# Four buffers for weight halves, gate columns carried in the first z group, v and o groups 512 wide, Q and K normalised together

## The chip, the core and the metric

One Trainium2 chip, one of its cores. The metric is device microseconds of one execution of the whole program: the median of several executions, beside one more execution that is profiled.

## What is computed

One layer of a hybrid decoder over 256 tokens of width 2048, in float32. Four mixers run side by side on slices of one projection, then an output projection, then a SwiGLU block:

```python
def rmsnorm(x, w): return x * rsqrt(mean(x * x, -1) + eps) * w

u = rmsnorm(x, attn_norm) @ w_in          # w_in: 2048 x 6928
u_gdn, u_mlstm, u_rglru, u_rwkv = split(u)
# gated delta net: silu(conv(q, k, v)), l2norm(q), l2norm(k), gates a_raw, b_raw (4 + 4 columns),
#   chunkwise delta rule (a triangular solve per chunk), rmsnorm(o) * silu(z)
# mLSTM: silu(conv(q, k)), v, o, gates i_raw, f_raw (4 + 4 columns), rmsnorm(sigmoid(o) * h)
x = x + concat([y_gdn, y_mlstm, y_rglru, y_rwkv], -1) @ w_out      # 2048 x 2048
n = rmsnorm(x, ffn_norm)
x = x + (silu(n @ ffn_w_gate) * (n @ ffn_w_up)) @ ffn_w_down       # hidden 5632
return rmsnorm(x, final_norm)
```

## The kernel before

**Products in halves.** A float32 operand is split into a high part, rounded to the float32r format, and the rest as a low part. `mm3` (lines 169 to 171) makes one product of three matmuls: high x high, high x low, low x high. Weights come in units of 128 x 1024 float32 (512 KB). One unit goes through three engines: SP's queue loads it into a `raw` buffer (4 of them), ACT copies it to `whi`, DVE subtracts to `wlo` (3 of each), all recorded at line 274 because one helper issues them.

**Groups.** `group` (line 374) makes 256 columns of the input projection from four units: 96 matmuls that move 256 columns each, into one PSUM bank (`big`). The order in the program is: low-rank and R0, K0, V0, R1, K1, V1 of RWKV, four groups of RG-LRU, then of the gated delta net z0, Q0, K0, V0, z1, Q1, K1, V1, then of mLSTM v0, o0, q0, k0, v1, o1, q1, k1. Then come `w_out` and the feed-forward part, whose groups are 512 wide with two banks.

**Mixers.** The mixers are generators (`rwkv_half`, `rglru_half`, `gdn_half`, `mlstm_half`, `joint_solve`). `spawn` registers one, and `tick` lets each live generator take a step, 0.65 steps for each unit of weights. So their small matmuls (L409 products, L413 transposes, through `Lag`, with a lower priority) stand among the 96 matmuls of the groups. The order of each engine is fixed when the program is built: a scheduler with priorities lists it, and on the chip every engine goes through its list in that order and waits where an operand is not there. A buffer of a pool (`slots`: A, B and L of 2 KB a partition, D of 4 KB) that is still in use also makes an instruction wait, or move back in the list.

**The gates.** `gates_mm` makes the 16 gate columns of both mixers in a product of its own: 48 matmuls `mx<-nhi,sA` of 16 output rows and 256 columns.

**The delta rule's end.** `gdn_half` goes, after the triangular solve, through two chunks in turn: products with the state (L409), a subtract (L985), further products, squares for the norm (ACT L990), a power (POOL L993), the product with z's gate (L996) and the new state (L1019); then L413 transposes and a last ACT copy (L1038). mLSTM's half likewise makes K x Q, a product with a decay (L1065), products with V, and ends in POOL L1088 and transposes. `w_out` takes the eight parts in the order rw, rg, gd (`early`), for four column blocks q, and then ml (`late`); `split` (L1178 on ACT, L1179 on DVE) halves each part where it is first needed.

## Time and profile before

| | us |
|---|---|
| median of 3 executions | 1277.48 (1275.78 to 1279.14) |
| the profiled execution | 1275.4 |
| its span, first to last instruction | 1273.4 |
| TensorE (PE) busy in the span | 1241.5 |
| DVE (VectorE) busy | 780.7 |
| ACT (ScalarE) busy | 633.6 |
| POOL (GpSimd) busy | 112.3 |

2.0 us of the profiled execution lie around its span. Busy time of PE counts matmuls that stand in its pipeline, so PE can be busy and still not at its peak. A granted clock (PEclk) of 1.00 is 2.4 GHz; 0.51 is its lower level, 1.2 GHz. Groups of rows from the trace name an operation as out<-in by the names of the program, without numbers of buffers.

### The profile page before, as it was taken

The numbers are of one execution on the slowest core, as the hardware profiler recorded it, in microseconds if no ns is written. First come the engines' busy times: TensorE is split into PE (matmuls) and PEld (weight loads), VectorE is DVE, ScalarE is ACT, GpSimd is POOL, SyncE is SP. The second block draws the span as 40 slices with busy tenths as digits, with TensorE's granted clock in tenths as the row PEclk, the third lists the DMA queues.
The fourth block names the chain that finished last, engine by engine and source line by source line (L and its number), as shares of the span: only waits on it lengthen the run. The fifth ranks groups of instructions, "written<-read, shape, count | busy, mean of one in ns | idle before, by whom it ended". The sixth has DMA issues, their size and how long they took to land.

```text
span 1273.4 us, 18370 instructions
## 1 busy us (share of the span) xinstructions
PE 1241.5 (98%) x7216; PEld 1072.9 (84%) x7216; DVE 780.7 (61%) x1045; ACT 633.6 (50%) x831; POOL 112.3 (9%) x123
## 2 busy tenths in 40 slices
PE   9899999999899999999999999999999999999997
PEld 8788999988899788888888888888888888888885
DVE  7885799665689775744444444454445455557554
ACT  7664684526643454644444344444444444445443
POOL 1520210212401020000000000000000000001000
PEclk9999999999898999999999999999999999999999
DMA  8554436445455356566666666666666666666663
GB/s 320 187 169 133 143 109 191 136 127 160 134 169 156 117 166 191 176 189 188 187 194 189 190 191 206 199 194 191 190 186 197 185 185 194 198 191 190 197 190 125
DMA packets 72198, 226.97 MB, mean 178 GB/s; under 512 B 15752, under 2 KB 16016, under 8 KB 72112
## 3 DMA queue, kind: packets, MB, share of 16 engines
q1 hardware_dynamic: 71504, 224.14, 57.5%
q0 software_dynamic: 464, 1.57, 0.4%
q8 instruction: 56, 0.92, 0.3%
q14 instruction: 30, 0.25, 0.1%
q10 hardware_dynamic: 144, 0.10, 0.0%
HBM read 222.49 MB, written 3.28 MB: 177 GB/s over the span
## 4 chain that ended last, share of the span: by engine, by line
PE 85%; DVE 8%; issue 2%; ACT 2%; DMA 1%; POOL 1%; DVEq 0%; POOLq 0%; SPq 0%; ACTq 0%
PE big L171 13%; PE big L170 13%; PE big L169 13%; PE mx L170 10%; PE mx L171 10%; PE mx L169 10%; PE mx L409 4%; PE mxl L169 3%; PE mxl L171 3%; PE mxl L170 3%; DVE wlo L274 3%; PE big L277 2%; DVE sD L499 1%; DVE sD L500 1%; DVE sA L763 1%
## 5 line engine op out<-in xcount | busy, mean ns | idle before, releaser
L274 DVE TENSOR_TENSOR wlo<-raw,whi 128x1024 fp32r<-128x1024 f32 x396 | 488.4, 1234 | 375.0 <-ACT whi L274 374.0
L274 ACT ACTIVATE whi<-raw 128x1024 fp32r<-128x1024 f32 x396 | 418.7, 1057 | 456.3 <-PE big L171 280.6
L170 PE MATMUL big<-wlo,nhi 128*128 128x512 f32 (+1 forms) x464 | 163.3, 352 | 3.6 <-DVE wlo L274 3.6
L169 PE MATMUL big<-whi,nhi 128*128 128x512 f32 (+1 forms) x464 | 162.1, 349 | 0.7 <-ACT whi L274 0.7
L171 PE MATMUL big<-whi,nlo 128*128 128x512 f32 (+1 forms) x464 | 162.4, 350 | 0.0
L171 PE MATMUL big<-nhi,wlo 128*128 128x256 f32 x544 | 157.8, 290 | 3.6 <-DVE wlo L274 3.6
L170 PE MATMUL big<-nlo,whi 128*128 128x256 f32 x544 | 158.1, 291 | 0.0
L169 PE MATMUL big<-nhi,whi 128*128 128x256 f32 x544 | 157.6, 290 | 0.0
L169 PE MATMUL mx<-whi,nhi 128*128 128x512 f32 x352 | 138.0, 392 | 0.0
L171 PE MATMUL mx<-whi,nlo 128*128 128x512 f32 x352 | 137.0, 389 | 0.0
L170 PE MATMUL mx<-wlo,nhi 128*128 128x512 f32 x352 | 137.0, 389 | 0.0
L171 PEld LDWEIGHTS big<-nhi,wlo 128*128 128x128 f32 x544 | 104.9, 193 | 6.0 <-DVE wlo L274 4.4
L170 PEld LDWEIGHTS big<-nlo,whi 128*128 128x128 f32 x544 | 105.1, 193 | 2.2 <-issue 1.0
L169 PEld LDWEIGHTS big<-nhi,whi 128*128 128x128 f32 x544 | 105.0, 193 | 1.9 <-issue 0.7
L170 PEld LDWEIGHTS big<-wlo,nhi 128*128 128x128 f32 x464 | 89.7, 193 | 15.2 <-DVE wlo L274 4.0
L169 PEld LDWEIGHTS big<-whi,nhi 128*128 128x128 f32 x464 | 89.5, 193 | 11.6 <-ACT whi L274 0.9
L171 PEld LDWEIGHTS big<-whi,nlo 128*128 128x128 f32 x464 | 89.7, 193 | 10.8
L170 PE MATMUL mx<-wlo,sA 128*128 128x512 f32 x216 | 84.3, 390 | 0.1
L169 PE MATMUL mx<-whi,sA 128*128 128x512 f32 x216 | 84.4, 391 | 0.0
L171 PE MATMUL mx<-whi,sA 128*128 128x512 f32 x212 | 82.5, 389 | 0.0
L171 PEld LDWEIGHTS mx<-whi,nlo 128*128 128x128 f32 x352 | 66.1, 188 | 13.8
L170 PEld LDWEIGHTS mx<-wlo,nhi 128*128 128x128 f32 x352 | 66.1, 188 | 13.3
...
## 6 DMA issues: line engine op xcount, KB each, us to landing
...
```

Source lines behind the costliest of these rows:

```text
L169: i = nc.tensor.matmul(out, ahi, bhi, start=start, stop=False, skip_group_check=True)
L170: nc.tensor.matmul(out, ahi, blo, start=False, stop=False, skip_group_check=True)
L171: self.last_mm = nc.tensor.matmul(out, alo, bhi, start=False, stop=stop, skip_group_check=True)
L274: i = fn(*a, **k)
L277: i = fn(*a, **k)
L409: return self.em.nc.tensor.matmul(*a, **k)
L499: nc.vector.tensor_tensor(tv, col, row, op=ALU.mult)
L500: nc.vector.tensor_tensor(inv[:, j + 1 : n, 0:b], inv[:, j + 1 : n, 0:b], tv, op=ALU.add)
L763: nc.vector.scalar_tensor_tensor(o[:, d:T], u[:, 0 : T - d], tap[3 - d], o[:, d:T], op0=ALU.mult, op1=ALU.add)
```

## The change

Five edits. (1) `NHI` goes from 3 to 4: a fourth `whi` and `wlo`, paid with two A and two B slots. (2) The 16 gate columns are appended to the weights of the group z0, which becomes 272 wide, in six units of three or two K tiles (`token_group`, tokens as output rows); `gates_mm` now copies 16 columns out of each of the two banks and transposes them. (3) The mLSTM's v and o are made by two groups 512 wide for both halves, in place of four of 256, and ahead of them stand q0 and k0. (4) In `gdn_half`, Q's and K's normalisation run side by side, so that the two Ln stand together and the two Exp. (5) In `w_out`, a part is split one turn ahead of its use (`ready`), and ml's two parts before the late pass.

```diff
@@ -29,8 +29,8 @@
-SLOTS = dict(A=14, B=13, L=4, D=16)
-NRAW, NHI = 4, 3
+SLOTS = dict(A=12, B=11, L=4, D=16)
+NRAW, NHI = 4, 4
 
 
 RW, RG, GD, ML = OFF_RW, OFF_RG, OFF_GDN, OFF_ML
...
@@ -40,14 +40,20 @@
+ZG = GD + 1536
+ZG_UNITS = ((0, 3), (3, 3), (6, 3), (9, 3), (12, 2), (14, 2))
 
 
 def plan():
 
     units = []
-    cols = [RW + c for c in range(0, 1792, 256)] + [RG + c for c in range(0, 1024, 256)] + [o + c for o in (GD, ML) for c in range(0, 2048, 256)]
+    cols = [RW + c for c in range(0, 1792, 256)] + [RG + c for c in range(0, 1024, 256)] + [GD + c for c in range(0, 2048, 256)] + [ML + c for c in range(0, 1024, 256)]
     for c in cols:
-        units += [("w_in", k, 4, c, 256) for k in range(0, KT, 4)]
+        if c == ZG:
+            units += [("z_gates", k, nk, c, 272) for k, nk in ZG_UNITS]
+        else:
+            units += [("w_in", k, 4, c, 256) for k in range(0, KT, 4)]
+    units += [("w_in", k, 2, ML + c, 512) for c in (1024, 1536) for k in range(0, KT, 2)]
     units += [("w_out", k, 2, c, 512) for c in range(0, D, 512) for k in range(0, KT, 2)]
     for c in range(0, HID, 512):
         units += [(w, k, 2, c, 512) for w in ("ffn_w_gate", "ffn_w_up") for k in range(0, KT, 2)]
...
@@ -370,6 +377,22 @@
+
+    def token_group(self, name, col, n, units, pre=None):
+
+        banks = [self.bank(), self.bank()]
+        for u, (k0, nk) in enumerate(units):
+            w = self.weights(name, k0, nk, col, n)
+            if pre:
+                pre(u)
+            for a in range(2):
+                ts = slice(a * P, a * P + P)
+                for kk in range(nk):
+                    k = k0 + kk
+                    self.mm3(banks[a][:, 0:n], self.nhi[:, k, ts], self.nlo[:, k, ts], w[0][:, kk, :], w[1][:, kk, :], start=k == 0, stop=k == KT - 1)
+            if self.gens:
+                self.tick(TICKS * nk * n / UNIT)
+        return banks
 
     def group(self, name, col, tm=False, acts=None, pre=None):
 
...
@@ -770,37 +793,35 @@
...
-def gates_mm(em):
+def gates_mm(em, zg):
     nc = em.nc
-    gs = em.S()
-    ghi, glo = (gs.bitcast(F32R)[:, i * 256 : i * 256 + 256].rearrange("p (k n) -> p k n", k=KT) for i in range(2))
-    nc.scalar.activation(ghi, em.gw, AF.Copy)
-    nc.vector.tensor_tensor(glo, em.gw, ghi.bitcast(F32), op=ALU.subtract)
+    gt = em.S()
+    with em.tc.high_priority(offset=EPRIO):
+        for a in range(2):
+            nc.vector.tensor_copy(gt[:, a * 16 : a * 16 + 16], zg[a][:, 256:272])
     z = em.mx()
     o = z[0:16, 0:T]
-    for k in range(KT):
-        em.mm3(o, ghi[:, k, :], glo[:, k, :], em.nhi[:, k, :], em.nlo[:, k, :], start=k == 0, stop=k == KT - 1)
-    em.free(gs)
+    for a in range(2):
+        em.pe.transpose(z[0:16, a * P : a * P + P], gt[:, a * 16 : a * 16 + 16], em.ident)
+    em.free(gt)
     g = em.S(2)
     gp = em.gp
     U, V = g[0:16, 0:T], g[0:16, T : 2 * T]
...
@@ -870,15 +890,30 @@
     nc = em.nc
     KQ = em.S(2)
     KQv = KQ.rearrange("p (s n) -> p s n", s=2)
-    for s, X, bias in ((1, Q, em.c_lnq), (0, K, 0.0)):
+    sqs, parts = [], []
+    for X in (Q, K):
         silu2(em, X)
-        sq = em.S()
-        nc.scalar.activation(sq, X, AF.Square)
-        z = yield from sums(em, em.onesr, sq)
-        rsqrt_ln(em, sq, z, em.c_4eps, ebias=bias)
+    for X in (Q, K):
+        sqs.append(em.S())
+        nc.scalar.activation(sqs[-1], X, AF.Square)
+    for sq in sqs:
+        parts.append((em.S(c="B"), em.S(c="B")))
+        nc.scalar.activation(parts[-1][0].bitcast(F32R), sq, AF.Copy)
+        nc.gpsimd.tensor_tensor(parts[-1][1].bitcast(F32R), sq, parts[-1][0], op=ALU.subtract)
+    yield
+    zs = []
+    for p in parts:
+        zs.append(em.mx())
+        for i in range(2):
+            em.pe.matmul(zs[-1], em.onesr, p[i].bitcast(F32R), start=i == 0, stop=i == 1)
+        em.free(*p)
+    for sq, z in zip(sqs, zs):
+        nc.scalar.activation(sq, z, AF.Ln, bias=em.c_4eps)
+    for s, X, sq, bias in ((1, Q, sqs[0], em.c_lnq), (0, K, sqs[1], 0.0)):
+        nc.scalar.activation(sq, sq, AF.Exp, scale=-0.5, bias=bias)
         nc.vector.tensor_tensor(KQv[:, s, :], X, sq, op=ALU.mult)
         em.free(sq, X)
-        yield
+    yield
     silu2(em, V)
     z = em.mx()
     for u in range(4):
...
@@ -1192,14 +1227,19 @@
     row = {"gd": 0, "ml": 4, "rg": 8, "rw": 12}
     sp = {}
 
+    def ready(m, hf):
+        if (m, hf) not in sp:
+            while (m, hf) not in em.mix:
+                em.tick()
+            sp[m, hf] = split(em, em.mix[m, hf])
+            em.free(em.mix[m, hf])
+
     def run(q, parts):
         banks = [em.bank(), em.bank()]
         for i, (m, hf) in enumerate(parts):
-            if (m, hf) not in sp:
-                while (m, hf) not in em.mix:
-                    em.tick()
-                sp[m, hf] = split(em, em.mix[m, hf])
-                em.free(em.mix[m, hf])
+            ready(m, hf)
+            if (m, hf) in early and q == 0 and i + 1 < len(early):
+                ready(*early[i + 1])
             hi, lo = (t.bitcast(F32R) for t in sp[m, hf])
             whi, wlo = em.weights("w_out", row[m] + 2 * hf, 2, q * 512, 512)
             for a in range(2):
...
@@ -1216,6 +1256,9 @@
     late = [("ml", 0), ("ml", 1)]
     for q in range(4):
         run(q, early)
+        if q == 2:
+            ready("ml", 0)
+    ready("ml", 1)
     ss = em.const([P, 2, 4], "ss1")
 
     def norm(q):
...
@@ -1409,31 +1439,41 @@
                 Gt = gelu2(em, grp(RG + 512 + 256 * hf))
                 em.spawn(f"rg{hf}", rglru_half(em, hf, X, Gt, wax))
         if "gd" in parts or "ml" in parts:
-            em.spawn("gates", gates_mm(em))
             em.gnh = em.const([P, 1], "gnh")
             nc.vector.tensor_scalar(em.gnh, em.PT["gdn_norm"], 0.5, None, op0=ALU.mult)
         if "gd" in parts:
             for hf in range(2):
-                z = grp(GD + 1536 + 256 * hf, tm=True)
                 SZ = em.S(c="L")
-                silu2(em, SZ, z)
+                if hf == 0:
+                    zg = em.token_group("z_gates", ZG, 272, ZG_UNITS)
+                    for a in range(2):
+                        silu2(em, SZ[:, a * T : a * T + T], zg[a][:, 0:T])
+                    em.spawn("gates", gates_mm(em, zg))
+                else:
+                    silu2(em, SZ, grp(ZG + 256, tm=True))
                 Q, K, V = (conv(em, grp(GD + 512 * i + 256 * hf), em.PT["gdn_conv"], 12, (4 * i + 2 * hf, 4 * i + 2 * hf + 1)) for i in range(3))
                 em.spawn(f"gd{hf}", gdn_half(em, hf, Q, K, V, SZ))
                 if hf == 0:
                     em.spawn("gds", joint_solve(em, "gd", 64, 32, 8, True))
         if "ml" in parts:
+            qk = [conv(em, grp(ML + 512 * i), em.PT["mlstm_conv"], 8, (4 * i, 4 * i + 1)) for i in range(2)]
+            v1s = [em.S(2) for _ in range(2)]
+            V1 = [t[:, 0:516].rearrange("p (a h n) -> p a h n", a=2, h=2) for t in v1s]
+            b = em.token_group("w_in", ML + 1024, 512, PAIRS)
             for hf in range(2):
-                v1s = em.S(2)
-                V1 = v1s[:, 0:516].rearrange("p (a h n) -> p a h n", a=2, h=2)
-                nc.gpsimd.memset(V1[:, :, :, 128:129], 1.0)
-                b = grp(ML + 1024 + 256 * hf, tm=True)
-                nc.scalar.activation(V1[:, :, :, 0:128], b.rearrange("p (a h n) -> p a h n", a=2, h=2), AF.Copy)
-                b = grp(ML + 1536 + 256 * hf, tm=True)
-                SO = em.S(c="L")
-                nc.scalar.activation(SO, b, AF.Tanh, scale=0.5)
-                nc.vector.tensor_scalar(SO, SO, 0.5, 0.5, op0=ALU.mult, op1=ALU.add)
-                Q, K = (conv(em, grp(ML + 512 * i + 256 * hf), em.PT["mlstm_conv"], 8, (4 * i + 2 * hf, 4 * i + 2 * hf + 1)) for i in range(2))
-                em.spawn(f"ml{hf}", mlstm_half(em, hf, Q, K, V1, SO, v1s))
+                nc.gpsimd.memset(V1[hf][:, :, :, 128:129], 1.0)
+                for a in range(2):
+                    nc.scalar.activation(V1[hf][:, a, :, 0:128], b[a][:, hf * T : hf * T + T].rearrange("p (h n) -> p h n", h=2), AF.Copy)
+            b = em.token_group("w_in", ML + 1536, 512, PAIRS)
+            SO = [em.S(c="L") for _ in range(2)]
+            for hf in range(2):
+                for a in range(2):
+                    nc.scalar.activation(SO[hf][:, a * T : a * T + T], b[a][:, hf * T : hf * T + T], AF.Tanh, scale=0.5)
+                nc.vector.tensor_scalar(SO[hf], SO[hf], 0.5, 0.5, op0=ALU.mult, op1=ALU.add)
+            for hf in range(2):
+                if hf:
+                    qk = [conv(em, grp(ML + 512 * i + 256), em.PT["mlstm_conv"], 8, (4 * i + 2, 4 * i + 3)) for i in range(2)]
+                em.spawn(f"ml{hf}", mlstm_half(em, hf, *qk, V1[hf], SO[hf], v1s[hf]))
```

`token_group` replaces the feed-forward part's own nested `group`, with the same matmuls; `silu2` takes narrower sources. Each unit is loaded with as many columns as it has.

On PE, in the delta net's first z group (nhi, nlo: the halves of the normalised tokens; mx_2045: the gates' bank; sA_275: the gates' weight halves), the order before is:

```order
L169 MATMUL big_1980<-whi_1983,nhi 128x256
L170 MATMUL big_1980<-wlo_1984,nhi 128x256
L171 MATMUL big_1980<-whi_1983,nlo 128x256
L409 MATMUL mx_2021<-sA_243_1799,sD_162_1283 128x256 x2
L409 MATMUL mx_2026<-sA_243_1799,sD_162_1283 128x256
L169 MATMUL mx_2045<-nhi,sA_275_2042 16x256
L170 MATMUL mx_2045<-nlo,sA_275_2042 16x256
L171 MATMUL mx_2045<-nhi,sA_275_2042 16x256
```

and of the change, at the same place:

```order
L176 MATMUL big_1980<-whi_1983,nhi 128x272
L177 MATMUL big_1980<-wlo_1984,nhi 128x272
L178 MATMUL big_1980<-whi_1983,nlo 128x272
L176 MATMUL big_1979<-whi_2007,nhi 128x272
L177 MATMUL big_1979<-wlo_2008,nhi 128x272
L178 MATMUL big_1979<-whi_2007,nlo 128x272
```

The 48 rows of 16x256 are gone, and the 96 of the group are 272 wide.

On ACT, where the RWKV's last norm runs (sB_448, sB_451 before, sB_455, sB_458 after; mx: the sums it takes its roots of; in mLSTM's first group before), the order before is:

```order
L486 ACT_TABLE_LOAD
L486 ACTIVATE sB_448_3516<-mx_3638,cv 128x512
L759 ACTIVATE sA_473_3648<-big_3485,chan 128x256
L487 ACT_TABLE_LOAD
L487 ACTIVATE sB_448_3516<-sB_448_3516 128x512
L486 ACT_TABLE_LOAD
L486 ACTIVATE sB_451_3522<-mx_3643,cv 128x512
L274 ACTIVATE whi_3793<-raw_3791 128x1024
L487 ACT_TABLE_LOAD
L487 ACTIVATE sB_451_3522<-sB_451_3522 128x512
L274 ACTIVATE whi_3825<-raw_3823 128x1024
```

and of the change:

```order
L509 ACT_TABLE_LOAD
L509 ACTIVATE sB_455_3484<-mx_3606,cv 128x512
L509 ACTIVATE sB_458_3490<-mx_3611,cv 128x512
L782 ACTIVATE sA_480_3616<-big_3453,chan 128x256
L510 ACT_TABLE_LOAD
L510 ACTIVATE sB_455_3484<-sB_455_3484 128x512
L510 ACTIVATE sB_458_3490<-sB_458_3490 128x512
L898 ACTIVATE sA_488_3673<-sA_430_3260 128x512
L898 ACTIVATE sA_489_3675<-sA_450_3444 128x512
L901 ACTIVATE sB_490_3677<-sA_488_3673 128x512
L281 ACTIVATE whi_3799<-raw_3797 128x1024
```

Four table loads among the RWKV norm's rows have become two; two more follow for the delta net's half in either kernel.

On PE, where the delta net's chain ends and the output projection begins (big_4901, big_4648: the bank of k1; big_5113, big_4893: the first of w_out; mx: the mixers' banks), before:

```order
L171 MATMUL big_4901<-nhi,wlo_5046 128x256
L409 MATMUL mx_5021<-sA_652_4936,sD_361_2834 128x128 x2
L409 MATMUL mx_5026<-sB_505_3861,sA_575_4427 128x128
L169 MATMUL big_5113<-whi_5121,sA_682_5115 128x512
L409 MATMUL mx_5026<-sB_505_3861,sA_575_4427 128x128
L409 MATMUL mx_5031<-sB_638_4872,sB_511_3901 128x128
L170 MATMUL big_5113<-wlo_5122,sA_682_5115 128x512
L171 MATMUL big_5113<-whi_5121,sA_683_5116 128x512
L409 MATMUL mx_5031<-sB_634_4868,sB_519_3965 128x128
```

and of the change:

```order
L432 MATMUL mx_4713<-sA_505_3787,sA_530_3957 128x256
L432 MATMUL mx_4713<-sA_505_3787,sA_530_3957 128x128
L432 MATMUL mx_4777<-sD_653_4683,sD_369_2803 128x128 x2
L432 MATMUL mx_4782<-sB_512_3835,sA_576_4238 128x128 x2
L432 MATMUL mx_4787<-sA_636_4602,sB_518_3875 128x128
L432 MATMUL mx_4799<-sD_531_3966,sD_659_4708 128x129 x3
L432 MATMUL mx_4846<-sB_397_2990,sA_584_4285 128x128
L432 MATMUL mx_4787<-sA_632_4598,sB_526_3939 128x128
L432 MATMUL mx_4787<-sA_636_4602,sB_518_3875 128x128
L432 MATMUL mx_4787<-sA_632_4598,sB_526_3939 128x128
L432 MATMUL mx_4846<-sB_397_2990,sA_584_4285 128x128
```

From the chain's first 64x64 product to its last rows, 33 matmuls of k1 and 28 of w_out stand among its rows before, and 4 of w_out after. The mLSTM's K x Q products (mx_4713 and, ahead, mx_4522), which stood within v1 before, stand in this chain too.

On DVE, the second row of w_out's first split (sA_690) stands in the change behind the second chunk of the delta net's second half:

```order
L1027 TENSOR_SCALAR gss_4600<-gss_4600 128x2
L786 SCALAR_TENSOR_TENSOR sA_682_4876<-big_4648,chan,sA_682_4876 128x255
L1031 SCALAR_TENSOR_TENSOR sA_633_4599<-mx_4787,grs_4601,sL_354_2739 128x128
L1031 SCALAR_TENSOR_TENSOR sA_633_4599<-mx_4787,grs_4601,sL_354_2739 128x128
L1119 TENSOR_SCALAR mss_4515<-mss_4515 128x2
L786 SCALAR_TENSOR_TENSOR sA_682_4876<-big_4648,chan,sA_682_4876 128x254
L1020 TENSOR_SCALAR sB_649_4679<-mx_4846,GT 128x128
L786 SCALAR_TENSOR_TENSOR sA_682_4876<-big_4648,chan,sA_682_4876 128x253
L1020 TENSOR_SCALAR sB_649_4679<-mx_4846,GT 128x128
L1214 TENSOR_TENSOR sA_690_4896<-sB_465_3530,sA_689_4895 128x512
```

Before, the same row (L1179, sA_683) stands ahead of the first chunk's new state:

```order
L996 SCALAR_TENSOR_TENSOR sB_635_4869<-mx_4882,grs_4871,sL_391_3025 128x128
L996 SCALAR_TENSOR_TENSOR sB_635_4869<-mx_4882,grs_4871,sL_391_3025 128x128
L1179 TENSOR_TENSOR sA_683_5116<-sB_461_3592,sA_682_5115 128x512
L1019 SCALAR_TENSOR_TENSOR sB_505_3861<-mx_4956,neg,sB_505_3861 128x128
L1019 SCALAR_TENSOR_TENSOR sB_505_3861<-mx_4956,neg,sB_505_3861 128x128
L1019 SCALAR_TENSOR_TENSOR sB_389_3021<-mx_5021,neg,sB_389_3021 128x128
```

It has moved past the whole of the first chunk and the subtracts of the second.

## Rows read from the trace of the kernel before

**Rows 1.** The page: busy time of each engine, its share of the span, instructions.

```profile
PE 1241.5 (98%) x7216; PEld 1072.9 (84%) x7216; DVE 780.7 (61%) x1045; ACT 633.6 (50%) x831; POOL 112.3 (9%) x123
```

**Rows 2.** Stretches: us, then busy us of PE, PEld, DVE, ACT, POOL; PEclk, DMA, GB/s.

```profile
309.90:411.60 101.70, 94.07 (x716) 92.10 (x715) 81.81 (x151) 54.20 (x76) 25.60 (x23) 0.93 0.48 148
411.60:447.50 35.90, 33.33 (x306) 28.96 (x304) 26.59 (x63) 17.02 (x38) 3.17 (x4) 1.00 0.38 118
...
520.00:1260.00 740.00, 739.86 (x3323) 613.20 (x3322) 387.94 (x362) 342.91 (x392) 9.57 (x9) 1.00 0.63 189
```

**Rows 3.** PE's timeline (start us, us): the gates' first matmul, and the next after their last.

```profile
172.55 0.47 PE L169 MATMUL mx<-nhi,sA 128*16 128x256 f32 x1
...
178.89 0.28 PE L169 MATMUL big<-whi,nhi 128*128 128x256 f32 x1
```

**Rows 4.** PE's timeline: neighbours 256 wide, and 512 wide.

```profile
376.10 0.28 PE L170 MATMUL big<-wlo,nhi 128*128 128x256 f32 x1
376.22 0.28 PE L171 MATMUL big<-whi,nlo 128*128 128x256 f32 x1
...
799.69 0.39 PE L169 MATMUL mxl<-whi,nhi 128*128 128x512 f32 x1
799.92 0.39 PE L170 MATMUL mxl<-wlo,nhi 128*128 128x512 f32 x1
```

**Rows 5.** PE's timeline from 310 to 340 us: rows with an idle time before them.

```profile
313.50 0.51 PE L409 MATMUL mx<-sA,exact 128*128 128x512 f32 x1 [0.59 <-POOL sA L422]
324.67 0.58 PE L170 MATMUL big<-wlo,nhi 128*128 128x256 f32 x1 [3.62 <-DVE wlo L274]
334.29 0.39 PE L169 MATMUL big<-whi,nhi 128*128 128x256 f32 x1 [0.68 <-ACT whi L274]
```

**Rows 6.** ACT's and DVE's timelines ahead of the longest of these waits.

```profile
320.10 1.28 ACT L487 ACT_TABLE_LOAD   x1
...
311.07 1.23 DVE L274 TENSOR_TENSOR wlo<-raw,whi 128x1024 fp32r<-128x1024 f32 x1 [0.28 <-ACT whi L274]
...
322.05 1.43 DVE L741 TENSOR_TENSOR sB<-sB,sB 128x512 f32<-128x512 f32 x1 [1.91 <-ACT sB L487]
323.41 1.21 DVE L274 TENSOR_TENSOR wlo<-raw,whi 128x1024 fp32r<-128x1024 f32 x1
```

**Rows 7.** Two stretches with the lower clock, columns as in rows 2.

```profile
323.70:330.60 6.90, 5.93 (x26) 5.74 (x27) 5.34 (x5) 3.31 (x5) 6.20 (x4) 0.51 0.36 105
381.70:388.60 6.90, 6.11 (x26) 5.93 (x27) 6.55 (x12) 1.68 (x3) 0.00 (x0) 0.51 0.49 153
```

**Rows 8.** PE's timeline: two more waits, and a product of mLSTM's first half.

```profile
192.38 0.41 PE L413 MATMUL mx<-ident,sD 16*128 16x16 f32 x4 [1.02 <-DVE sD L819]
...
382.49 1.22 PE L409 MATMUL mx<-sA,sA 128*128 128x256 f32 x2 [2.75 <-DVE sA L774]
...
395.32 0.60 PE L409 MATMUL mx<-sA,sA 128*128 128x256 f32 x2
```

**Rows 9.** PE's timeline at the end of the delta rule's chain.

```profile
425.22 0.96 PE L409 MATMUL mx<-sA,sA 64*64 64x64 f32 x16
...
447.63 0.50 PE L171 MATMUL big<-whi,sA 128*128 128x512 f32 x1 [0.15 <-DVE sA L1179]
```

**Rows 10.** Groups of DVE and POOL, 425.2 to 447.5; the last row 440 to 480.

```profile
L274 DVE TENSOR_TENSOR wlo<-raw,whi 128x1024 fp32r<-128x1024 f32 x4 | 4.9, 1219 | 1.6 <-ACT whi L274 1.6
L1179 DVE TENSOR_TENSOR sA<-sB,sA 128x512 fp32r<-128x512 f32 x4 | 2.7, 683 | 0.0
L985 DVE TENSOR_SCALAR sA<-mx,GT 128x128 f32<-128x128 f32 x4 | 1.4, 346 | 1.5 <-PE mx L409 1.5
L763 DVE SCALAR_TENSOR_TENSOR sA<-big,chan,sA 128x255 f32<-128x255 f32 x2 | 0.9, 473 | 0.0
...
L993 POOL TENSOR_TENSOR grs<-gss,mhalf 128x2 f32<-128x2 f32 x4 | 3.2, 791 | 32.7 <-DVE gss L992 32.7
...
L1088 POOL TENSOR_SCALAR sB<-sB,mrs 128x128 f32<-128x128 f32 x4 | 4.5, 1133 | 0.2
```

More of the change, by code (lines that the diff above doesn't have):

```diff
@@ L55, in plan @@
     return units
+PAIRS = [(k, 2) for k in range(0, KT, 2)]
 UNIT_AT = {u: i for i, u in enumerate(plan())}
@@ L779, in gates_load @@
     nc, A = em.nc, em.A
[L780 to L782 removed]
+    em.rs16 = em.wu.bitcast(F32)[0:16, :]
     gp = em.const([16, 4], "gp")
```

45 lines of the change are left out of this document (15 added, 30 removed).

## The prediction

> **What bounds the kernel now.** I read the page's busy times first: PE has 98% of the span, DVE 61%, ACT 50% [rows 1]. Next came the stretches, since a share over the whole span hides where PE waits. From 520 us on PE is busy in 739.86 of 740.00 us [rows 2]; the change leaves that part as it is, so nothing is won or lost there. The two stretches ahead of it are where PE falls short: 94.07 of 101.70 us, at a mean clock of 0.93, in the mLSTM's groups, and 33.33 of 35.90 us where k1 ends and w_out begins [rows 2]. So a gain must come from work that PE no longer has, from the waits of these stretches, or from the clock that falls behind such waits.
>
> A change of under 0.3%, 3.8 us, can hardly be told from no change in this kernel.
>
> **1. Less work on PE.** The gates' product is 48 matmuls. Neighbours 256 wide start 0.12 us apart (376.10, 376.22), neighbours 512 wide 0.23 (799.69, 799.92) [rows 4]; over five neighbours the latter is 0.2267. So a column costs (0.2267 - 0.120) / 256 = 0.417 ns and a matmul 13.3 ns on top. The 48 are worth 48 x 0.120 = 5.8 us; they stand between 172.55 and 178.89, 6.3 us with a little other work among them [rows 3]. In their place 96 matmuls of z0 get 16 more columns, 96 x 16 x 0.417 ns = 0.6, and two transposes come, 0.2 by the price of a 256-wide matmul each: -4.9 us.
>
> v and o: a pair of groups has 192 matmuls 256 wide (23.0 us), now 96 of 512 (21.8): -1.3, and twice that is -2.6. Together **-7.5 us**.
>
> A rule speaks against the second part. The Trainium skill, "TensorE: Matmul & The Clock Gate", section "Wait — 56ns, not 53.3ns?", gives a warm start-to-start of the columns at 2.4 GHz and about 2.5 ns on top. By it the wide groups would save 192 x 2.5 ns, some 0.5 us in both pairs, and the sum would come out 2 us higher. The trace shows 13.3 ns for these matmuls with their own loads of stationary operands [rows 4], so the trace decides here.
>
> **2. The wait at 320 us.** Ahead of its rows at 313.50, 324.67 and 334.29 PE waits 0.59, 3.62 and 0.68 us, the longest time for a wlo [rows 5]. DVE writes none between 311.07 and 323.41, because the row ahead of it, L741, waits 1.91 us for ACT's Exp, and ACT is loading its tables in turn for Ln and Exp, 1.28 us a time [rows 6]. In the new order the two Ln stand together and the two Exp, so two of six loads are gone, 2.6 us of ACT; the fourth wlo lets one more unit be ready ahead. Neither does it wholly: the wlo rows still stand behind the norm's rows on DVE. I walked through the new order with these durations and found 1.5 us of wait left (0 to 5 as bounds, from all hidden to as now). 0.59 + 3.62 + 0.68 = 4.9, so **-3.4 us**.
>
> **3. The clock behind it.** From 323.70 to 330.60 the granted clock is 0.51, the 1.2 GHz level, right behind PE's idle time [rows 7]. Half of 6.9 us, 3.4, is lost there. A wait of 1.5 us may still bring it; the idle times of 0.59 and 1.02 [rows 5, 8] are not all followed by a fall. I take 7 in 10 of it: **-2.4** (0 to -3.4).
>
> **4. The wait at 379 us.** PE waits 2.75 us for DVE's K of the mLSTM's first half (L774) [rows 8], since the K x Q product stands in v1's group while DVE is full with the delta net's solve. In the new order q0 and k0 come ahead of v and o, their silu stands ahead of the solve on DVE, and the product itself stands behind k1. Nothing is late in its place there: **-2.8**. The stretch 381.70 to 388.60 at 0.51 [rows 7] is its consequence, **-3.4**. The lower bound of both is nothing: the solve's own rows still fill DVE, and its wlo could be what is late.
>
> **5. The end of the delta rule's chain.** This is the term that counts against. Before, the chain's steps run among dense matmuls: from 425.22 to 447.63 [rows 9] PE has 33 matmuls of k1 and 28 of w_out to do while it waits for DVE, ACT and POOL. From the start of k1 (411.6) it has 35.9 us; 96 x 0.12 + 28 x 0.2267 = 17.9 of them are projection, 18.0 the mixers' products and waits. In the new order nearly all of k1 stands ahead of the chain, and only 4 matmuls of w_out among it, because the second row of the first split stands on DVE behind the second chunk of the second half. With two A slots and two B slots fewer, the split's target comes free late. So PE must wait out the chain.
>
> How long is that? From the first 64x64 product to that split, DVE has 49 rows: 9 of the conv kind (0.47), 3 of 512 wide (0.68), one wlo (1.22), and 36 others, which I price at L985's 0.346 [rows 10]: 4.2 + 2.0 + 1.2 + 12.5 = 20 us. That is the lower bound, with DVE never idle. Walking through it in order adds the round trips DVE has to wait for: PE's products, ACT's copies, and above all one POOL queue in which four powers of 0.79 and four products of 1.13 [rows 10] stand in turn, so that the second half's power waits behind the mLSTM's two products. That walk gives 26.8 us. Ahead of it, k1 to the chain's start takes 14.5 (11.5 of matmuls, 3.0 of mixers). So k1 and the chain take 41.3; dense work in them is 96 x 0.12 + 4 x 0.2267 = 12.4, and 3.3 are mLSTM products (from such rows as 395.32 [rows 8]) that stood elsewhere before. The rest is 25.6 against 18.0: **+7.6 us** (with the lower bound of 20, +0.8). I take the walk, because every step of it is a row with a duration, and DVE's rows wait on a chain that no other order relieves.
>
> Such a wait can also cost clock, as the two of rows 7 show: nothing to 3.4 us; PE has many short products in between, so I take **+2**.
>
> **6. At nothing.** The 272-wide units make ACT's copies and DVE's subtracts 0.7 us longer over the group; in z0 PE is the bound. v's banks are emptied by four ACT copies in place of two; o's second bank may wait for the third (0 to 1 us), behind 21.8 us of matmuls. SP has one load more in a queue that runs ahead by four buffers. The gates now follow z0, and the wait of 1.02 at 192.38 [rows 8] may move with them, in either direction. What hides them is PE's backlog; if that cover went, all together would be 2 us. The start (0 to 60 us) is bound by DVE, which a fourth wlo gives no time.
>
> **The sum.** -7.5 - 3.4 - 2.4 - 2.8 - 3.4 + 7.6 + 2 = -9.9 us. The profiled execution took 1275.4, so it would take 1265.5; the median of the runs, 1277.5, lies 2.1 above that execution. Against the median I forecast **1267 us** (1267.6 by the sum).
>
> **The rivals.**
>
> *The chain costs little* (0.22). If DVE runs through its 49 rows without waiting, term 5 is +0.8 and the clock doesn't fall: -19.5 + 0.8 = -18.7, 1259 us. For it: in 411.60 to 447.50 DVE is busy 26.59 of 35.90, so it works most of the time in such a chain now. Against it: the order holds PE's rows to the chain's.
>
> *The chain costs more than all that is won* (0.12). Its place is the same, PE between k1's last matmul and w_out's third; the price is that of the second chunk's round trips not overlapping at all with the first half's. It decides from a loss of 19.5 us on, 15.7 already means no change that can be told; it would need a chain of 35 to 39 us, half as long again as the walk, with the clock low throughout. 25 us lost would give 1283. Half of the chance goes to no change and half to slower.
>
> *The waits only move* (0.20). Terms 2 to 4 give nothing, because the solve and the norm still fill DVE and another wlo is late: -7.5 + 7.6 + 2 = +2.1, 1279.6, and 1271 with the cheap chain. For it: in 309.90 to 411.60 DVE is busy 81.81 of 101.70 us [rows 2], with the same work after the change. Against it: the waits of 3.62 and 2.75 have causes that the new order takes away. A quarter of it is faster, a half same, a quarter slower.
>
> *Wide groups save nothing* (0.04): each matmul costs its columns alone, term 1 is -5.5, the sum -7.9, 1269.6. The trace's starts speak against it [rows 4]. The page named in part 1 would have it so, and the trace does not agree.
>
> **How the numbers follow.** My forecast has 0.42, for 1262 to 1272. Faster by over 0.3% (below 1273.7): 0.42 + 0.22 + 0.05 + 0.04 = 0.73. Same: 0.06 + 0.10 = 0.16, and 0.01 of the forecast's upper edge, 0.17. Slower (above 1281.3): 0.06 + 0.05, less 0.01 for rounding, 0.10. The range reaches from 1255, below the cheap chain with the start a little better, to 1279, where most of the case of moved waits lies; the case above it and what lies below leave out about 0.15.
>
> **What would show it.** Step 1: no rows of 16x256, wide rows 0.227 apart. Steps 2 to 4: in the mLSTM's groups no wait of PE above 2 us, and a granted clock of 1.00 throughout. Step 5: k1 to steady w_out 41 us, with PE idle for some 12, waiting for DVE's split row and the chain's products. The prediction is wrong if that stretch takes 36 or 50, or if a wait for wlo of over 3 us is still there ahead of it.

## The result: slower by 1.3%

The change takes 1294.37 us in the median of four runs (1291.05 to 1298.07), the kernel before 1277.61: a ratio of 1.0133, with a 95% interval of 1.0101 to 1.0164. The forecast was 1267, with a range from 1255 to 1279. The time lies outside it, and on the other side of the kernel before.

The page of the changed kernel, busy times and the slices of PE and its clock (32.3 us each):

```profile
PE 1242.5 (96%) x6978; PEld 1066.5 (83%) x6978; DVE 781.3 (60%) x1049; ACT 632.1 (49%) x836; POOL 110.4 (9%) x123
...
PE   9899999999798899999999999999999999999997
...
PEclk9998999999899799999999999999999999999998
```

The span is 1291.7 us, 18.3 longer than before. PE is as busy as before [rows 1] with 238 matmuls fewer, and idle for 49.2 us in place of 31.9. The mean granted clock of the span is 0.979 in place of 0.990. So the matmuls are gone, and more than their time has come back as waiting and as a lower clock.

Where: the starts of the groups on PE, before and after, cut the span into five stretches.

| stretch | before, us | after, us | change | forecast |
|---|---|---|---|---|
| start to z0 | 168.6 | 173.3 | +4.8 | 0 |
| z0 to the mLSTM's first group | 141.3 | 136.4 | -5.0 | -4.9 |
| mLSTM's groups, to k1 | 101.7 | 97.5 | -4.3 | -17.9 |
| k1 to the feed-forward part | 122.7 | 145.4 | +22.6 | +12.9 |
| the rest of the span | 739.0 | 739.2 | +0.2 | 0 |

The forecasts of the third and fourth rows hold the 3.3 us of mLSTM products that part 5 of the prediction moves from the one stretch to the other. Up to the mLSTM's first group almost nothing is won: it starts at 309.70, before at 309.90. The -5.0 of the second row goes with the +4.8 of the first.

Here is the third stretch (first row, against the first of [rows 2]) and then the fourth, cut as in the prediction at the chain's first 64x64 product and at steady w_out; the second and third rows together stand against the second of [rows 2], whose columns these are:

```profile
309.70:407.16 97.46, 87.39 (x504) 77.88 (x503) 77.81 (x133) 50.87 (x68) 17.95 (x14) 0.93 0.51 151
407.16:431.86 24.70, 21.33 (x187) 19.45 (x185) 11.68 (x22) 4.25 (x5) 0.00 (x0) 0.72 0.51 155
431.86:457.98 26.12, 17.74 (x114) 15.49 (x114) 16.23 (x51) 10.90 (x38) 6.92 (x10) 0.82 0.09 31
457.98:552.51 94.53, 93.55 (x434) 77.27 (x433) 61.44 (x84) 47.76 (x78) 8.51 (x9) 0.99 0.56 167
```

From the chain's first 64x64 product to steady w_out it takes 26.1 us, where the walk had 26.8. But k1 to that product takes 24.7, where the prediction had 14.5, with the clock at 0.72. Together that is 50.8 us, in place of 41.3. The PE rows around it:

```profile
415.86 0.60 PE L432 MATMUL mx<-sB,sB 32*32 32x32 f32 x8 [3.37 <-DMA sB<-dr]
...
443.53 2.04 PE L432 MATMUL mx<-sB,sA 128*128 128x128 f32 x8 [4.33 <-DVE sB L1020]
...
451.44 0.50 PE L176 MATMUL big<-whi,sA 128*128 128x512 f32 x1
```

Before, the first of these rows stands at nearly the same time, behind a shorter wait:

```profile
415.11 0.41 PE L409 MATMUL mx<-sB,sB 32*32 32x32 f32 x8 [0.93 <-DMA sB<-dr]
```

PE waits 3.37 us for the transfer that brings the solve's result back, and 4.33 for the chain; w_out's first matmul is at 451.44, against 435.37 before. Around the idle times the clock is low (the first of the three stretches lies in the mLSTM's groups):

```profile
325.90:336.10 10.20, 5.84 (x26) 5.75 (x27) 6.02 (x10) 4.27 (x7) 4.23 (x3) 0.50 0.39 129
414.60:428.20 13.60, 12.34 (x103) 11.16 (x104) 4.16 (x8) 2.11 (x2) 0.00 (x0) 0.50 0.42 130
441.90:448.70 6.80, 5.17 (x22) 5.02 (x23) 3.94 (x15) 2.68 (x11) 2.60 (x4) 0.50 0.00 0
```

At this clock neighbours 256 wide start 0.213 us apart, in place of 0.120 [rows 4]:

```profile
416.98 0.41 PE L176 MATMUL big<-nhi,whi 128*128 128x256 f32 x1
417.20 0.41 PE L177 MATMUL big<-nlo,whi 128*128 128x256 f32 x1
```

So some 0.44 of PE's busy time there is lost: about 5.4 of the 12.34 us in the second of the three stretches, an estimate from these two spacings.

Why PE waits there is on DVE: the last rows of the solve and the copy that is sent, after and then before.

```profile
408.14 0.18 DVE L523 TENSOR_TENSOR sD<-sD,sD 32x31 f32<-32x31 f32 x1
408.36 1.12 DVE L526 COPY sD<-sD 32x1024 f32<-32x1024 f32 x1
```

```profile
408.55 1.17 DVE L503 COPY sD<-sD 32x1024 f32<-32x1024 f32 x1
```

The solve ends at the same time in both, to 0.2 us, though PE has k1 4.5 us earlier. It starts later: its first row is at 368.28, before at 356.50. The way there, on POOL, DVE and PE of the changed kernel:

```profile
324.10 2.24 POOL L767 TENSOR_TENSOR sB<-sB,sB 128x512 f32<-128x512 f32 x1
326.42 1.59 POOL L768 TENSOR_TENSOR sB<-sB,sB 128x512 f32<-128x512 f32 x1
327.97 2.24 POOL L902 TENSOR_TENSOR sB<-sA,sB 128x512 fp32r<-128x512 f32 x1
```

```profile
324.19 0.73 PE L432 MATMUL mx<-sB,exact 128*128 128x512 f32 x2 [2.74 <-POOL sB L902]
...
330.26 0.79 PE L432 MATMUL mx<-sB,exact 128*128 128x512 f32 x1 [4.99 <-POOL sB L902]
...
348.56 0.59 PE L432 MATMUL mx<-sD 128*128 128x256 f32 x2
...
353.11 1.20 PE L432 MATMUL mx<-sD 128*128 128x256 f32 x2 [2.35 <-DVE sB L950]
```

```profile
351.85 0.35 DVE L1092 TENSOR_SCALAR sD<-sA,ccol 128x256 f32<-128x256 f32 x1 [2.68 <-DMA sA<-Md]
352.12 0.47 DVE L786 SCALAR_TENSOR_TENSOR sA<-big,chan,sA 128x253 f32<-128x253 f32 x1
352.51 0.34 DVE L949 SCALAR_TENSOR_TENSOR sB<-mx,nbeta,sA 128x128 f32<-128x128 f32 x1
```

The second low part of the joint normalisation (L902) stands on POOL behind the RWKV's products, and PE waits 4.99 us for it, after 2.74 for the first. The second half's K x Q products are at 348.56 (before at 334.95), and their reader on DVE, L949, stands behind a row of the mLSTM that waits 2.68 us for a transfer. With 2.35 us ahead of the row at 353.11, PE is idle for 10.1 us in the mLSTM's stretch, against 7.6 before [rows 5, 8], and the mean clock is 0.93 in both.

The wide matmuls are as forecast: 0.227 us from one to the next.

```profile
374.12 0.39 PE L177 MATMUL big<-wlo,nhi 128*128 128x512 f32 x1
374.34 0.39 PE L178 MATMUL big<-whi,nlo 128*128 128x512 f32 x1
374.57 0.39 PE L176 MATMUL big<-whi,nhi 128*128 128x512 f32 x1
```

### The profile page after: what moved, and what is told of

It is laid out like the page before. It is cut to its first block, busy times and chain, and to the rows that moved or that the text cites. A ratio compares the mean times of both kernels' runs of the same rounds, so it can differ in the third digit from the quotient of the medians.

```text
span 1291.7 us, 17897 instructions
## 1 busy us (share of the span) xinstructions
PE 1242.5 (96%) x6978; PEld 1066.5 (83%) x6978; DVE 781.3 (60%) x1049; ACT 632.1 (49%) x836; POOL 110.4 (9%) x123
## 4 chain that ended last, share of the span: by engine, by line
PE 88%; DVE 6%; POOL 2%; issue 2%; DMA 1%; ACT 1%; DVEq 0%; POOLq 0%; SPq 0%; ACTq 0%
PE big L178 14%; PE big L177 13%; PE big L176 13%; PE mx L176 10%; PE mx L178 10%; PE mx L177 10%; PE mx L432 5%; PE mxl L176 3%; PE mxl L178 3%; PE mxl L177 3%; DVE wlo L281 2%; PE big L284 2%; DVE sD L522 1%; DVE sD L295 1%; PE mx L436 1%
## 5 line engine op out<-in xcount | busy, mean ns | idle before, releaser
L281 DVE TENSOR_TENSOR wlo<-raw,whi 128x1024 fp32r<-128x1024 f32 x398 | 494.5, 1244 | 380.2 <-ACT whi L281 379.3
L178 PE MATMUL big<-nhi,wlo 128*128 128x256 f32 x544 | 160.9, 296 | 5.5 <-DVE wlo L281 5.5
L178 PE MATMUL big<-whi,nlo 128*128 128x512 f32 (+2 forms) x400 | 150.5, 376 | 0.0
L177 PE MATMUL big<-wlo,nhi 128*128 128x512 f32 (+2 forms) x400 | 150.1, 375 | 0.0
L176 PE MATMUL big<-whi,nhi 128*128 128x512 f32 (+2 forms) x400 | 149.8, 375 | 0.0
L176 PEld LDWEIGHTS big<-nhi,whi 128*128 128x128 f32 x544 | 107.9, 198 | 2.0 <-issue 0.7
L178 PEld LDWEIGHTS big<-whi,nlo 128*128 128x128 f32 x400 | 75.7, 189 | 13.3
L177 PEld LDWEIGHTS big<-wlo,nhi 128*128 128x128 f32 x400 | 75.5, 189 | 13.3
L176 PEld LDWEIGHTS big<-whi,nhi 128*128 128x128 f32 x400 | 75.5, 189 | 13.2
L176 PE MATMUL mx<-whi,sA 128*128 128x512 f32 x212 | 82.9, 391 | 0.7 <-ACT sA L1213 0.7
L178 PE MATMUL mx<-whi,sA 128*128 128x512 f32 x208 | 80.9, 389 | 0.0
```

What stands on the lines that cost most here:

```text
L176: i = nc.tensor.matmul(out, ahi, bhi, start=start, stop=False, skip_group_check=True)
L177: nc.tensor.matmul(out, ahi, blo, start=False, stop=False, skip_group_check=True)
L178: self.last_mm = nc.tensor.matmul(out, alo, bhi, start=False, stop=stop, skip_group_check=True)
L281: i = fn(*a, **k)
```

## The experiments

All ratios are to the kernel before, which was run again beside each (medians from 1276.7 to 1278.1), with 95% intervals. Edits have the numbers of the section on the change. Stretches are read from one profiled execution of each run.

| run | edits in it | median, us | ratio |
|---|---|---|---|
| the change | 1 2 3 4 5 | 1294.4 | 1.0133 (1.0101 to 1.0164) |
| e1_undo_buffers | 2 3 4 5 | 1282.8 | 1.0039 (1.0025 to 1.0054) |
| e1b_slots_only | 2 3 4 5, slots of 1 | 1289.3 | 1.0090 (1.0075 to 1.0105) |
| e3_undo_ml_order | 1 2 4 5 | 1292.9 | 1.0120 (1.0104 to 1.0136) |
| e4_undo_norm | 1 2 3 5 | 1294.4 | 1.0131 (1.0115 to 1.0147) |
| e5_undo_ready | 1 2 3 4 | 1289.2 | 1.0107 (1.0063 to 1.0150) |
| l234_no_buffers_no_ready | 2 3 4 | 1283.0 | 1.0041 (1.0027 to 1.0054) |
| l23_gates_wide | 2 3 | 1284.4 | 1.0055 (1.0016 to 1.0094) |
| w_vo_first | 2 3, v and o first | 1290.1 | 1.0101 (1.0084 to 1.0118) |
| l2_gates_only | 2 | 1278.8 | 1.0017 (1.0007 to 1.0027) |
| b1_buffers_only | 1 | 1284.5 | 1.0065 (1.0040 to 1.0090) |
| b4_norm_only | 4 | 1277.6 | 0.9999 (0.9988 to 1.0010) |
| b5_ready_only | 5 | 1275.9 | 0.9985 (0.9974 to 0.9996) |
| s1_split_in_d | 1 2 3 4 5, other slots | 1288.9 | 1.0083 (1.0052 to 1.0114) |
| s2_split_in_d_no_buffers | 2 3 4 5, other slots | 1279.7 | 1.0014 (0.9992 to 1.0036) |
| b45_norm_ready | 4 5 | 1274.7 | 0.9971 (0.9951 to 0.9990) |

### One edit undone

The theories at the start: A, that the missing slots hold back w_out's first splits; B, that the joint normalisation has moved k1 ahead of the chain.

```diff
-SLOTS = dict(A=12, B=11, L=4, D=16)
-NRAW, NHI = 4, 4
+SLOTS = dict(A=14, B=13, L=4, D=16)
+NRAW, NHI = 4, 3
```

> The change with three whi/wlo and the old slot counts (A 14, B 13), the other four edits kept. Theory A (the two slots fewer in A and B hold back w_out's first splits, so PE waits out the delta rule's chain): 23 matmuls of w_out stand in the chain in place of 16, the stretch from k1's first matmul to the first of the feed-forward part falls from 145.4 us to about 133, and the time from 1294 to about 1280. Theory B (k1 has run ahead of the chain because Q and K are normalised together, whatever the slots): 16 matmuls of k1 stay in the chain, the stretch stays at 142 to 147 and the time at 1290 to 1297. The RWKV stage, 4.8 us longer after the change, goes back to before's length if the buffers are its cause.

Measured: 1282.8, 11.6 us under the change. z0 starts at 169.1 again, and k1 to the feed-forward part takes 139.9 us, neither theory's number: 5.4 less than in the change, 17.2 more than before. On POOL the joint normalisation's subtraction (L902) now stands ahead of the RWKV's products, and PE doesn't wait for it; a wait of 4.03 us for a wlo, ahead of the row at 324.49, is there in its place.

```profile
317.82 1.29 POOL L902 TENSOR_TENSOR sB<-sA,sB 128x512 fp32r<-128x512 f32 x1 [7.54 <-DVE sB L764]
320.14 1.26 POOL L767 TENSOR_TENSOR sB<-sB,sB 128x512 f32<-128x512 f32 x1 [1.03 <-DVE sB L766]
```

So the waits for L902 take edit 4 and the fewer slots together.

```diff
-    sqs, parts = [], []
-    for X in (Q, K):
-        silu2(em, X)
...
+    for s, X, bias in ((1, Q, em.c_lnq), (0, K, 0.0)):
+        silu2(em, X)
+        sq = em.S()
+        nc.scalar.activation(sq, X, AF.Square)
+        z = yield from sums(em, em.onesr, sq)
```

> The change with Q and K normalised one after the other again, the other four edits kept. Theory B: the two waits of PE for POOL at 321 and 325 us (2.7 and 5.0) and the 10.2 us at the lower clock behind them go, 40 matmuls of k1 stand in the chain in place of 16, its stretch falls from 145 to about 135, and the time from 1294 to 1275 to 1282. Theory A: only the two waits and their clock go, 10 to 13 us, but the stretch from k1 on stays at 143 to 147: 1281 to 1285.

Measured: 1294.4, no gain at all, and outside both ranges. The place of PE's waits in the profile moves: in place of L902, 2.90 for ACT at 325.68, 2.54 and 1.70 for DVE behind it, and the transfer of the solve's result is waited for longer:

```profile
417.88 0.60 PE L432 MATMUL mx<-sB,sB 32*32 32x32 f32 x8 [4.92 <-DMA sB<-dr]
...
443.58 2.05 PE L432 MATMUL mx<-sB,sA 128*128 128x128 f32 x8 [4.96 <-DVE sB L1005]
```

Theory B falls: with 40 matmuls of k1 back in the chain, that stretch still takes 143.4 us. Theory A has the stretch right, but not the 10 to 13 us that were to be won ahead of it.

```diff
-            if (m, hf) in early and q == 0 and i + 1 < len(early):
-                ready(*early[i + 1])
...
-        if q == 2:
-            ready("ml", 0)
-    ready("ml", 1)
```

> The change with each part split where it is first needed again, the other four edits kept. If splitting a turn ahead ties w_out's first matmuls to the chain, 24 matmuls of w_out stand in the chain in place of 16 and the time falls by 3 to 10 us to 1284 to 1291. By theories A and B this edit is worth nothing at the chain: 1292 to 1297.

Measured: 1289.2; the four executions spread from 1284 to 1296. A gain of a few us, not settled by this run alone; without the buffers the edit is worth nothing (l234 1283.0, e1 1282.8).

```diff
-            b = em.token_group("w_in", ML + 1024, 512, PAIRS)
...
+                b = grp(ML + 1024 + 256 * hf, tm=True)
...
-            b = em.token_group("w_in", ML + 1536, 512, PAIRS)
...
+                b = grp(ML + 1536 + 256 * hf, tm=True)
```

> The change with the mLSTM's v and o in 256-wide groups and in the old order (v0, o0, q0, k0, v1, o1, q1, k1), the other four edits kept. PE has 2.6 us more matmul time. If the new order of the mLSTM groups is what moves k1 ahead and puts the mLSTM's products into the chain, the stretch from k1 on falls by 10 us or more and the time to 1280 to 1288. By theory B only the 2.6 us are added and the wait at 379 us comes back with its clock (up to 6): 1294 to 1303.

Measured: 1292.9, between the two ranges. The wait at 379 us is back (3.76 at 382), 2.6 us of matmul time too, and the stretch from k1 on is 9.1 us shorter: the parts cancel.

### Built up from the kernel before

```diff
-            em.spawn("gates", gates_mm(em))
...
+                    zg = em.token_group("z_gates", ZG, 272, ZG_UNITS)
+                    em.spawn("gates", gates_mm(em, zg))
```

> The kernel before with the gate columns in z0 alone. PE loses 4.9 us of work well ahead of the delta rule's solve, whose start and end move with it. If the gain reaches the end, 1271 to 1273 against before's 1277; if the work between there and the solve's end is bound by DVE, the solve's end stays at 408 us and the time at 1275 to 1278.

Measured: 1278.8, just above the second range. Even z0's own stretch is shorter by 0.7 us only, and not by 4.9. Before (first) and with edit 2 (second), from z0's first matmul to that of the next group, columns as in [rows 2]:

```profile
168.50:187.50 19.00, 19.00 (x154) 17.48 (x154) 18.25 (x39) 17.38 (x26) 3.52 (x3) 1.00 0.30 99
```

```profile
169.10:187.40 18.30, 15.45 (x106) 14.87 (x106) 17.65 (x37) 16.66 (x24) 3.66 (x3) 0.91 0.42 127
```

```profile
184.76 0.59 PE L176 MATMUL big<-wlo,nhi 128*128 128x272 f32 x1 [2.85 <-DVE wlo L280]
```

DVE is busy for 18.25 of 19.00 us there, with the RWKV's solve. The gates' product mostly filled time in which PE would have waited for DVE. Without it PE waits 2.85 us for a wlo, and the mean clock of the stretch is 0.91.

```diff
+            qk = [conv(em, grp(ML + 512 * i), em.PT["mlstm_conv"], 8, (4 * i, 4 * i + 1)) for i in range(2)]
...
+            b = em.token_group("w_in", ML + 1024, 512, PAIRS)
...
+            b = em.token_group("w_in", ML + 1536, 512, PAIRS)
```

> The kernel before with the gate columns in z0 and the new mLSTM groups (q0 and k0 first, v and o 512 wide). Theory C: with q0 and k0 ahead of v and o their convolutions stand on DVE ahead of the second half's K x Q rows, so the solve starts 10 us later after the start of the mLSTM's groups (57 in place of 47), its end doesn't move, and PE waits for it: PE reaches k1 6 to 10 us earlier and gives it back, 1276 to 1284. If the order of the groups costs nothing: 1267 to 1270, as the work on PE falls by 7.5 and the wait at 379 goes.

Measured: 1284.4, slower by 5.6 than with the gates alone, though the executions spread (1282.9 to 1292.4) and the two intervals meet. The solve starts 53 us after the mLSTM's first group and ends at 403.6, PE has k1 at 403.6 (before: 411.6) and takes 138.4 us from there to the feed-forward part, 15.7 more than before. As theory C says, PE is early and gives it back; but the solve's end did move, by 4.6.

The same two edits with v and o ahead of q0 and k0:

```diff
-            qk = [conv(em, grp(ML + 512 * i), ...
...
+                qk = [conv(em, grp(ML + 512 * i + 256 * hf), em.PT["mlstm_conv"], 8, (4 * i + 2 * hf, 4 * i + 2 * hf + 1)) for i in range(2)]
```

> Edits 2 and 3 with v and o, 512 wide, ahead of q0 and k0, so that the convolutions come later on DVE, all else as before. If it is the place of q0 and k0 that makes the solve start late (theory C), the solve starts some 47 to 52 us after the mLSTM's first group in place of 53 and the time is 1274 to 1279, against 1284 with q0 and k0 first. If it is that PE has its work done too early whatever the order (the solve's end stays at 404 to 410 us and PE waits there), 1280 to 1287: in this order all of k1 stands ahead of the chain's 64x64 products.

Measured: 1290.1, above both ranges. The solve starts 47.6 us after the first group, as expected, and yet ends where it ended before (the copy behind it is at 409.03); PE, with k1 at 404.95, waits 2.05 us for its result, 3.7 for the chain, and is at the lower clock for most of 417 to 448. So it isn't the start of the solve that costs. In each of these orders PE is ready before the solve's result.

And the whole change without edits 1 and 5:

```diff
-SLOTS = dict(A=12, B=11, L=4, D=16)
-NRAW, NHI = 4, 4
+SLOTS = dict(A=14, B=13, L=4, D=16)
+NRAW, NHI = 4, 3
...
-                ready(*early[i + 1])
```

> Edits 2, 3 and 4: the change without the fourth buffers (slots as before) and without the early splits. If the two undone edits add up (11.6 and 5 us), 1277 to 1279. If they are two names for one thing, w_out's first splits waiting for slots, 1281 to 1284 as with the buffers alone undone.

Measured: 1283.0. Against l23 (1284.4) edit 4 is worth nothing that can be told, against e1 (1282.8) edit 5 neither. Then the slots apart from the fourth buffers, with all other edits of the change:

```diff
-NRAW, NHI = 4, 4
+NRAW, NHI = 4, 3
```

> The change with three whi/wlo but with the smaller slot counts (A 12, B 11), all other edits kept; 8 KB a partition stay unused. If the missing slots are what the buffers' edit costs, 1291 to 1297, as the whole change. If the fourth pair of buffers is (its unit is copied and subtracted ahead of the mixers' rows on ACT and DVE), 1280 to 1285, as with both undone.

Measured: 1289.3, between the two: the slots are 6.5 of the 11.6 us, the fourth buffers the other 5.1, if they are taken out in this order.

### Single edits, and other slots for the splits

Edits 1, 4 and 5 each alone on the kernel before.

```diff
-SLOTS = dict(A=14, B=13, L=4, D=16)
-NRAW, NHI = 4, 3
+SLOTS = dict(A=12, B=11, L=4, D=16)
+NRAW, NHI = 4, 4
```

> The kernel before with edit 1 alone: four whi/wlo, A 12 and B 11 slots. If the edit costs by itself (mixers' rows wait for slots, w_out's first splits stand behind the chain: 12 matmuls of w_out are left in the chain in place of 28), 1283 to 1290 against 1277. If it costs only together with the new order of the mLSTM's groups, 1275 to 1279.

Measured: 1284.5. The edit costs 6.7 us by itself. w_out's first matmul is at 447.33 (before: 435.37), and the stretch from k1 on takes 129.0 us, 6.2 more than before.

```diff
-        z = yield from sums(em, em.onesr, sq)
-        rsqrt_ln(em, sq, z, em.c_4eps, ebias=bias)
...
+    for sq, z in zip(sqs, zs):
+        nc.scalar.activation(sq, z, AF.Ln, bias=em.c_4eps)
```

> The kernel before with edit 4 alone, Q and K of the delta net normalised together. The chain at w_out keeps its order (43 matmuls of k1, 28 of w_out among its rows). If two table loads less shorten the wait of 3.6 us at 320 us and its clock, 1270 to 1275. If PE then waits for POOL's two subtractions in turn, as in the full change (5.0 us), 1276 to 1282.

Measured: 1277.6, no difference. The wait at 320 us is 4.07 in place of 3.62. But this run doesn't tell what two table loads less are worth: it still has six between 316 and 334 us (at 316.23, 318.59, 320.54, 323.49, 328.36 and 333.79), as before, and the subtractions on POOL stand ahead of the RWKV's products. Edit 4 removes two loads only beside edit 1.

```diff
+            ready(m, hf)
+            if (m, hf) in early and q == 0 and i + 1 < len(early):
+                ready(*early[i + 1])
```

> The kernel before with edit 5 alone, each part split a turn ahead. The waits of PE for the splits' subtract are 1.7 us in all before: if they go, 1274 to 1276. If the early splits only move them, 1276 to 1279.

Measured: 1275.9, 1.9 under before, which its interval just tells from it.

Then the direct test of the slots, with the whole change and without edit 1:

```diff
-def split(em, t, n=512):
+def split(em, t, n=512, c="A"):
...
-    hi, lo = em.S(), em.S()
+    hi, lo = em.S(c=c), em.S(c=c)
...
-            sp[m, hf] = split(em, em.mix[m, hf])
+            sp[m, hf] = split(em, em.mix[m, hf], c="D" if (m, hf) in (("rw", 0), ("rw", 1)) else "A")
```

> The whole change, with the halves of the two RWKV parts in D slots, which are long free, in place of A slots. w_out's first matmul stands 25 rows earlier, right behind the chain's first 64x64 products, and 11 to 17 of its matmuls stand among the chain's rows in place of 4. If it is slots that hold back w_out's first splits, k1 to the feed-forward part falls from 145.4 to 136 to 141 us, the lower clock behind 441 us goes, and the time is 1284 to 1290. If PE would wait there anyway, since the chain alone sets the end, 1292 to 1297.

> The change without the fourth buffers (three whi/wlo, A 14, B 13), with the halves of the two RWKV parts in D slots. 24 matmuls of w_out stand in the chain ahead of its transposes. If slots hold the splits back here too, 1275 to 1280 against 1282.8 without the D slots; if not, 1281 to 1285.

Measured: 1288.9 and 1279.7, 5.4 and 3.1 us less than without the D slots, both in the range for slots. The executions spread widely (1281.8 to 1295.7 and 1275.3 to 1286.3), and both intervals overlap those of the runs without D slots. In the first of the two w_out now starts among the chain's products:

```profile
426.79 1.67 PE L432 MATMUL mx<-sA,sA 64*64 64x64 f32 x13
428.39 0.50 PE L176 MATMUL big<-whi,sD 128*128 128x512 f32 x1
```

and its stretch from k1 on, columns as in [rows 2]:

```profile
405.62:542.25 136.63, 126.61 (x730) 106.63 (x729) 88.32 (x156) 63.24 (x119) 15.75 (x19) 0.98 0.48 149
```

The stretch from k1 on falls from 145.4 to 136.6 us, at a mean clock of 0.98; the execution profiled took 1283.3, 5.6 under the median, so a part of this is its own luck. That w_out starts 23 us earlier (428.39 for 451.44) shows that the splits did wait for slots; what it is worth in time is shown less well.

Last, edits 4 and 5 together on the kernel before (the two diffs above).

> The kernel before with edits 4 and 5 alone, no new buffers, the old gates and the old mLSTM groups. Each alone was 1277.6 (4) and 1275.9 (5) against 1277.8: if they add, 1275 to 1277, not told from before by 0.3%.

Measured: 1274.7, 3.4 under before in these runs, about the 0.3% that can be told. By its interval it is under both kernels; so is edit 5 alone, by less.

The profiles can also be lined up at the copy that sends the solve's result, here to the first product of the feed-forward part:

| run | copy, us | feed-forward part, us | between |
|---|---|---|---|
| before | 408.55 | 534.35 | 125.8 |
| l2_gates_only | 412.37 | 537.65 | 125.3 |
| b1_buffers_only | 411.26 | 542.52 | 131.3 |
| l23_gates_wide | 403.85 | 542.00 | 138.2 |
| the change | 408.36 | 552.51 | 144.2 |
| s1_split_in_d | 406.80 | 542.25 | 135.5 |
| s2_split_in_d_no_buffers | 401.24 | 534.66 | 133.4 |

The copy moves by 11 us over these runs, but the way behind it by 19. Two things go with the longer way. In l23, the change, s1 and s2, 43 of k1's 96 matmuls stand on PE ahead of the row that waits for the result, and 20 before and in l2. And w_out's first matmul comes 20 to 27 us behind the copy before and in l2, s1 and s2, but 36 to 43 behind it in the others.

## Why the prediction was wrong

**Part 1, the gates (-4.9).** The step that fails is the cover. The matmuls went and the price per matmul is right, but DVE sets the stretch: it is busy for 18.25 of 19.00 us. I priced a PE term there. Alone the edit makes the kernel 0.17% slower (ratio 1.0017), about 2 us. In the whole change z0's stretch is 5.2 us shorter, but it starts 4.8 later, and ends at 187.10 in place of 187.51. In the same 19 us DVE is as busy as before:

```profile
168.50:187.50 19.00, 19.00 (x149) 18.58 (x147) 18.45 (x39) 16.04 (x25) 4.71 (x4) 1.00 0.46 141
```

So up to z0's end 0.4 us are won, and that the second stretch meets its -4.9 is luck.

**Part 1, wide v and o (-2.6).** The price per matmul holds: 0.227 us for 512 columns. The rule of the Trainium skill weighed there ("TensorE: Matmul & The Clock Gate", section "Wait — 56ns, not 53.3ns?") would have 0.216, and the trace does not agree. The time isn't won, because PE comes to the solve's result early.

**Parts 2 and 3, the wait at 320 us and its clock (-5.8).** Wrong. PE waits 2.74 and 4.99 us for POOL's L902 in place of 3.62 for wlo, and 10.2 us are at the lower clock in place of 6.9. Two table loads did go, as forecast. The step that fails is that I walked the new order on ACT and DVE and not on POOL, where the two subtractions of the joint normalisation stand behind the RWKV's products. Undoing edit 4 changes nothing in the time: other waits take the place. With the old slots L902 stands ahead of the products, but there the six loads and the wait for a wlo (4.03) are back; so what the loads alone are worth stays open. Of a stretch at the lower clock I had taken half as lost, where the spacing above gives 0.44 of PE's busy time.

**Part 4, the wait at 379 us (-6.2).** Right as far as it goes: the wait is gone from there. But parts 2 to 4 were to win 12.0 us in the mLSTM's stretch, and won nothing: PE's idle time went from 7.6 to 10.1 us and the mean clock stayed at 0.93. The 4.3 us that the stretch is shorter are less than the 5.9 of work that it no longer has (2.6 in v and o, 3.3 moved). This is the largest miss, 13.6 us. The rival of the moved waits had this outcome, though it named another wlo and not POOL, and its price, 1279.6, lies 14.8 under the time measured.

**Part 5, the chain (+7.6 and +2).** Right in sign, and in the idle time: some 12 us were expected, and 11.8 came (3.4 up to the chain's first product, 8.4 behind it). The size is wrong: 50.8 us in place of 41.3, beyond the 50 that I had named as a sign of being wrong. Two steps failed. The clause that k1 to the chain's start takes 14.5 us holds PE's work alone, though those rows wait for the solve's result, which came at 415.11 before and at 415.86 in the change; it took 24.7, of which 3.4 are that wait and some 5.4 the lower clock. In the seven other runs in which all of k1 stands ahead of that product (e1, e5, l23, l234, w, s1, s2) it took 19.2 to 26.4. And the clock's term of +2 is too small: by the spacing above, the three stretches of lower clock between k1 and steady w_out cost some 8 to 9 us. The chain itself came out at 26.1 for 26.8 with some of that clock in it, which the walk had not counted, so that agreement is in part luck.

**Part 6, the start at nothing.** Wrong by 4.8 us. PE waits 1.27 us ahead of the row at 95.56 and 1.63 at 149.46, in every profile with edits 1 and 2 together and in none with the old slots. The clock is low for 3.4 us at 63 and for 6.8 at 97, but that isn't edit 1's: the profile of edit 5 alone, whose rows up to z0 are those of the kernel before, has the same two stretches and reaches z0 at 171.1, while edit 1 alone reaches it at 169.1. So some 2 to 3 us of such a difference can lie between two executions of the same rows.

What the runs put on each edit: the buffers 11.6 us in the whole change and 6.7 alone, of which w_out's late splits are the part that the D slots point to; the new mLSTM groups 5.6 on top of the gates; the gates 1 to 3; edits 4 and 5 nothing or a small gain. The edits don't add up, so these are prices beside the others. How the fourth buffers themselves cost 5 us is open: the order of ACT and DVE changes throughout, and no run here takes one such move alone. How much of the 22.6 us is clock and how much waiting isn't separated by a run either: a run that fills PE's idle time with other products wasn't made, since each added row moves the rest of the order.
